# Seven block products in place of eight in part of two FFN down projections

## The chip, the cores and the metric

The program runs on one core of a Trainium2 chip. The core has TensorE for matrix products (called PE in the profile, with its weight loads listed apart as PEld), VectorE (DVE), ScalarE (ACT), GpSimd (POOL) and SyncE (SP), whose queue issues most of the DMAs. Each engine works through a queue of its own in order, and the engines wait for each other by semaphores. Products land in PSUM, eight banks of 128 partitions x 512 float32; everything else lives in SBUF, 128 partitions wide.

The metric is device time in microseconds for one execution of the whole program, as the median of several executions. Smaller is better. A TensorE product takes a stationary operand of 128 x 128 (the weights that PEld loads) and streams a moving operand of up to 512 columns past it.

## The reference

A decoder trunk of two layers on 512 tokens of width 1024, in float32. Layer 0 is a gated mixer, layer 1 is sliding-window attention; both are followed by the same kind of feed-forward block (FFN), which is where the change lies:

```python
def conv_ffn(xn, w_up, conv_w, conv_b, w_down):
    S = xn.shape[1]
    h = xn @ w_up
    hp = jnp.pad(h, ((0, 0), (CONV_WIDTH - 1, 0), (0, 0)))
    c = conv_b + sum(hp[:, t:t + S] * conv_w[t] for t in range(CONV_WIDTH))
    g, u = jnp.split(c, 2, axis=-1)
    return (jax.nn.silu(g) * u) @ w_down
...
        h = h + conv_ffn(rmsnorm(h, norm_ffn[i]), f_w_up[i], f_conv_w[i], f_conv_b[i], f_w_down[i])
```

`w_up` is 1024 x 5632 and `w_down` is 2816 x 1024 in each layer. After the FFN comes a gated per-layer embedding, and after layer 0 a shared key/value projection.

## The kernel before

**Layout.** Activations are kept transposed: a tile holds 128 features as partitions and the 512 tokens as columns. The residual stream `h` is eight such tiles. The 2816 inner features of an FFN are 22 tiles, numbered `j`.

**Three products for one.** Operands go into TensorE as float32r in two pieces: a high part (a cast) and a low part (the original less the cast). Each product of a weight block and an activation tile is three matmuls, high x high, high x low and low x high (`mm3`, lines 185 to 196), added up in PSUM. So each float32 block costs three weight loads and three passes of 512 columns.

**Weights.** Weight matrices come from HBM in *pieces* of up to 128 x 2048 float32 (1 MB), in one fixed order, into three raw buffers `r0` to `r2` used in turn (`load`, lines 130 to 141). `pump` (143 to 167) splits each piece into *units* of up to 1024 columns: ScalarE casts the high part `wh` (line 164), VectorE subtracts for the low part `wl` (line 165). There are four buffers each for `wh` and `wl` (`WBUFS`), and `chunk` (175 to 183) sends the splits four units ahead before it takes the units it needs. A split waits for TensorE to release a unit buffer; a DMA waits for the splits to release a raw buffer.

**The FFN** (`ffn`, 401 to 443) is done in three parts of 8, 7 and 7 inner tiles (`PARTS`). `up(j)` multiplies the gate and the value columns of tile `j` (2 x 24 matmuls of 512 columns, into two PSUM banks), and then runs the epilogue for each of the two: VectorE scales by the norm's factor (`hs`, line 417), ScalarE applies the first tap of the convolution (line 421), VectorE the two others (422 and 423); then SiLU on ScalarE (426), the product of the two on VectorE (427), and `split` (271 to 274) into the high and low operands `ah{j}` and `al{j}`. These live in nine slots of an arena. When the tiles of a part are done, and one tile of the next part has been computed ahead, `dense_add` (389 to 399) multiplies them by four pieces of `w_down`, 256 output features each: 2 x 3 matmuls of 512 columns for each inner tile, two PSUM banks, and two additions onto `h` by VectorE (397). In the last part each finished tile of `h` goes straight into the next norm (`norm.take`).

**The norm's factor** of an FFN takes a detour: `begin` and `rstd` send it through DRAM and back by two DMAs on GpSimd's queue while TensorE already runs the first `up`. The products are scaled afterwards, so TensorE doesn't wait for it, and VectorE does.

**The order.** The program is traced in the order in which the Python code runs; a scheduler then orders each engine's queue ahead of time, putting an instruction in when its inputs should be ready, and among several the one that was traced first. What the chip later makes of the waits doesn't change the order.

Of the kernel before, what the change touches and what calls it, by code (L numbers as in the profile page):

```python
# [8 lines left out]
F32 = mybir.dt.float32  # L9
# [10 lines left out]
NJ = FF // P  # L20
PARTS = [(0, 8), (8, 15), (15, 22)]
SLOTS = 9
# [26 lines left out]
def tile_yoco(ctx: ExitStack, tc: tile.TileContext, t, out: bass.AP, out_b: bass.AP):  # L49
# [7 lines left out]
    mp = ctx.enter_context(tc.tile_pool(name="mp", bufs=1))  # L57
    tp = ctx.enter_context(tc.tile_pool(name="tp", bufs=2))
    dram = ctx.enter_context(tc.tile_pool(name="dram", bufs=1, space=bass.MemoryType.DRAM))
# [6 lines left out]
    pieces, paired = [], set()  # L66

# [10 lines left out]
    def plan_cols(w, n_chunks, kk, cols=256, k0=0):  # L78
        for c in range(n_chunks):
            plan(w[c, :, k0 * cols : (k0 + kk) * cols], kk * cols, cols)  # L80

    def plan_pair(w, k0, k1, own=None):

        paired.add(len(pieces))
        plan(w[:, :, k0 * 256 : k1 * 256].rearrange("c p m -> p c m"), (k1 - k0) * S, S, own)

    def plan_ffn(l):
        for i, (j0, j1) in enumerate(PARTS):
            if i == 0:
# [8 lines left out]
            plan_cols(t["w_down"][l], 4, j1 - j0, k0=j0)  # L98

# [13 lines left out]
    plan_ffn(1)  # L113
    free = [j % SLOTS for j in range(NJ, NJ + 8)]
    for c in range(2):
# [4 lines left out]
    units = [(i, q, lo, n) for i, p in enumerate(pieces) for q, (lo, n) in enumerate(p[2])]  # L120
    raws, ready, splits = {}, {}, {}
    state = {"raw": 0, "unit": 0, "next": 0, "tags": [0, 1, 2], "turn": 0, "pt": 0, "sent": {}}

    def behind(ins, front):
# [3 lines left out]
                          reason="order")  # L128

    def load(upto, queue=nc.sync):  # L130
        while state["raw"] < min(upto, len(pieces)):
            j = state["raw"]
            a, m = pieces[j][:2]
            tags = state["tags"]
            r = wp.tile([P, 2 * UNIT], F32, tag=f"r{tags[state['turn'] % len(tags)]}", bufs=1, name=f"wraw{j}")
            state["turn"] += 1
            ins = queue.dma_start(r[:, :m].rearrange("p (c m) -> p c m", c=2) if j in paired else r[:, :m], a)
            for front in state["sent"].pop(j, []):
                behind(ins, front)
            raws[j] = r  # L140
            state["raw"] += 1

    def pump(upto):
        while state["unit"] < min(upto, len(units)):
# [10 lines left out]
            if i in paired:  # L155
# [28 lines left out]

    def mm3(ps, parts, xs, c0, n=P, first=True, last=True, lows_last=False):


        todo = []
        for (wh, wl, off), (xh, xl) in zip(parts, xs):
            hi, low = (w[:, off + c0 : off + c0 + n] for w in (wh, wl))  # L190
            todo.append([(hi, xh), (hi, xl), (low, xh)])
        if lows_last:
            todo = [[t[j] for t in todo for j in (0, 2)], [t[1] for t in todo]]
        todo = [x for t in todo for x in t]
        for j, (w, x) in enumerate(todo):
            nc.tensor.matmul(ps, w, x, start=first and j == 0, stop=last and j == len(todo) - 1)  # L196

# [191 lines left out]
    def dense_add(xs, kk, norm):  # L389

        for c in range(4):
            parts = chunk(256, kk)
            for j in range(2):
# [4 lines left out]
                if norm is not None:  # L398
                    norm.take(m)

    def ffn(l, norm, nxt):

# [3 lines left out]
        def up(j):  # L406
# [20 lines left out]
            nc.vector.tensor_mul(a, a, cs[1])  # L427
            hi = ap.tile([P, S], F32R, tag=f"ah{j % SLOTS}", name=f"ah{j}")
            lo = ap.tile([P, S], F32R, tag=f"al{j % SLOTS}", name=f"al{j}")
            split(a, hi, lo)  # L430
            return hi, lo

        act = [up(0)]
        pe = None
        for i, (j0, j1) in enumerate(PARTS):
            act += [up(j) for j in range(j0 + 1, j1)]
            last = j1 == NJ
            if last:
                pe = ple_in_rows() if l else ple_in(l)
            nact = [] if last else [up(j1)]  # L440
            dense_add(act, j1 - j0, nxt if last else None)
            act = nact
        return pe
# [199 lines left out]
    xkv, xq = nm.xs[0][0], nm.xs[1][0]  # L643
    at = ctx.enter_context(tc.tile_pool(name="at", bufs=1))


# [565 lines left out]
```

## Time and profile before

| | us |
|---|---|
| median of 3 executions | 1129.52 (1129.44 to 1129.74) |
| span of the profiled execution, first to last instruction | 1127.4 |
| TensorE busy in it | 1118.7 (99%) |
| VectorE busy | 753.9 (67%) |
| ScalarE busy | 511.7 (45%) |
| GpSimd busy | 105.8 (9%) |

A time of its own is not given for the profiled execution beside its span; the span lies 2.1 us under the median, which is what stands around the first and the last instruction.

In the groups of instructions, a row is one line of the code on one engine with one shape: count, total busy time, mean duration of one in ns, and what ended the idle time before them. TensorE's matmuls overlap, so their durations (389 ns for 512 columns) are longer than the distance from one start to the next, and that distance is what counts. The granted TensorE clock was 0.998 over the span.

| stage (layer 0) | us from the span's start |
|---|---|
| `up` 0 to 8 | 143.9 to 242.35 |
| down projection, part 1 (8 tiles) | 242.35 to 285.87 |
| `up` 9 to 15 | 285.87 to 362.03 |
| down projection, part 2 (7 tiles) | 362.03 to 400.11 |
| `up` 16 to 21, embedding product | 400.11 to 476.51 |
| down projection, part 3 (7 tiles) | 476.51 to 514.59 |

Layer 1 has the same stages from 705.06 on.

### The profile page before, as it was taken

How to read it: one execution, taken by the hardware profiler on the slowest of the kernel's cores; microseconds unless marked ns; L12 is line 12 of the kernel's file. 1: busy time of each engine (PE TensorE's matmuls, PEld its weight loads, DVE VectorE, ACT ScalarE, POOL GpSimd, SP SyncE). 2: the span in 40 equal slices, each digit the busy share in tenths (PEclk: the TensorE clock that was granted, in tenths of full speed). 3: DMA queues.
4: the chain of work that ended last, by engine and by line, in shares of the span. 5: the costliest groups of instructions: out<-in, count | busy, mean ns of one | idle time of the engine just before them, and what ended most of it. 6: DMA issues, size and time to landing. Idle time of an engine off the chain costs nothing.

```text
span 1127.4 us, 13285 instructions
## 1 busy us (share of the span) xinstructions
PE 1118.7 (99%) x5115; PEld 930.4 (83%) x5115; DVE 753.9 (67%) x1166; ACT 511.7 (45%) x808; POOL 105.8 (9%) x167
## 2 busy tenths in 40 slices
PE   9999999999999999999999999999999999999997
PEld 7888888888888888888888887888888888888886
DVE  6566438873577457656988997488736773675686
ACT  5634325541344234544656776255413432344543
POOL 2100210000000000012204451100000000000210
PEclk9999999999999999999999999999999999999999
DMA  9632313333232222333134224333222233224333
GB/s 323 102 117 75 112 47 112 112 112 112 75 103 83 100 107 89 99 112 112 49 101 131 76 57 154 111 106 105 99 110 96 82 103 112 78 86 144 111 101 80
DMA packets 35616, 118.29 MB, mean 105 GB/s; under 512 B 11800, under 2 KB 17440, under 8 KB 26080
## 3 DMA queue, kind: packets, MB, share of 16 engines
q1 hardware_dynamic: 34800, 116.19, 31.9%
q0 software_dynamic: 336, 0.79, 0.4%
q8 instruction: 40, 0.66, 0.3%
q10 hardware_dynamic: 416, 0.46, 0.1%
q14 instruction: 24, 0.20, 0.1%
HBM read 109.02 MB, written 2.11 MB: 99 GB/s over the span
## 4 chain that ended last, share of the span: by engine, by line
PE 95%; DVE 2%; issue 1%; ACT 1%; DMA 0%; POOLq 0%; POOL 0%; ACTq 0%
PE up L196 42%; PE d L196 25%; PE q L196 4%; PE gate L196 4%; PE u L196 4%; PE o L196 2%; PE gt L205 1%; PE v L205 1%; PE gt L206 1%; PE gt L207 1%; PE v L206 1%; PE v L207 1%; PE pin L196 1%; PE k L196 1%; PE s L613 1%
## 5 line engine op out<-in xcount | busy, mean ns | idle before, releaser
L165 DVE TENSOR_TENSOR wl<-wraw,wh 128x1024 fp32r<-128x1024 f32 (+1 forms) x198 | 238.1, 1205 | 117.9 <-ACT wh L164 117.6
L164 ACT CAST wh<-wraw 128x1024 fp32r<-128x1024 f32 (+2 forms) x197 | 201.3, 1026 | 233.2 <-PE d L196 129.9
L196 PE MATMUL up<-nf00h,wh 128*128 128x512 f32 x352 | 137.1, 390 | 0.0
L196 PE MATMUL up<-nf10h,wh 128*128 128x512 f32 x352 | 137.0, 389 | 0.0
L196 PE MATMUL up<-nf00h,wl 128*128 128x512 f32 x352 | 136.9, 389 | 0.0
L196 PE MATMUL up<-nf10h,wl 128*128 128x512 f32 x352 | 136.9, 389 | 0.0
L196 PE MATMUL up<-nf10l,wh 128*128 128x512 f32 x352 | 136.9, 389 | 0.0
L196 PE MATMUL up<-nf00l,wh 128*128 128x512 f32 x352 | 136.9, 389 | 0.0
L196 PE MATMUL d<-ah,wh 128*128 128x512 f32 x352 | 136.9, 389 | 0.0
L196 PE MATMUL d<-al,wh 128*128 128x512 f32 x352 | 136.9, 389 | 0.0
L196 PE MATMUL d<-ah,wl 128*128 128x512 f32 x352 | 136.9, 389 | 0.0
L421 ACT ACTIVATE c<-hs,vec 128x512 f32<-128x512 f32 x88 | 71.5, 815 | 91.6 <-DVE hs L417 89.4
L422 DVE SCALAR_TENSOR_TENSOR c<-hs,vec,c 128x511 f32<-128x511 f32 x88 | 65.7, 749 | 33.7 <-ACT c L421 33.6
L397 DVE TENSOR_TENSOR h<-h,d 128x512 f32<-128x512 f32 x56 | 38.4, 686 | 72.6 <-PE d L196 72.6
L196 PEld LDWEIGHTS up<-nf10h,wl 128*128 128x128 f32 x352 | 66.1, 188 | 13.8
L196 PEld LDWEIGHTS d<-ah,wh 128*128 128x128 f32 x352 | 66.1, 188 | 13.8
L196 PEld LDWEIGHTS up<-nf00h,wh 128*128 128x128 f32 x352 | 66.1, 188 | 13.7
L196 PEld LDWEIGHTS up<-nf00l,wh 128*128 128x128 f32 x352 | 66.1, 188 | 13.7
L196 PEld LDWEIGHTS d<-al,wh 128*128 128x128 f32 x352 | 66.1, 188 | 13.7
L196 PEld LDWEIGHTS d<-ah,wl 128*128 128x128 f32 x352 | 66.1, 188 | 13.7
L196 PEld LDWEIGHTS up<-nf10l,wh 128*128 128x128 f32 x352 | 66.1, 188 | 13.7
L196 PEld LDWEIGHTS up<-nf00h,wl 128*128 128x128 f32 x352 | 66.1, 188 | 13.7
(392 smaller groups left out, 1947.8 us busy)
## 6 DMA issues: line engine op xcount, KB each, us to landing
wraw<-in_w_up SPq DMA_DIRECT2D x44, 1024.0 KB, 4.8
wraw<-in_w_down SPq DMA_DIRECT2D x16, 896.0 KB, 4.6
wraw<-in_w_down SPq DMA_DIRECT2D x8, 1024.0 KB, 5.0
wraw<-in_w_gate SPq DMA_DIRECT2D x8, 1024.0 KB, 5.2
wraw<-in_w_u SPq DMA_DIRECT2D x4, 1024.0 KB, 8.0
wraw<-in_w_out SPq DMA_DIRECT2D x4, 1024.0 KB, 4.8
wraw<-in_w_q SPq DMA_DIRECT2D x4, 1024.0 KB, 5.2
wraw<-in_w_o SPq DMA_DIRECT2D x4, 1024.0 KB, 4.9
```

Of the source, the lines that this page charges most:

```text
L164: cast = nc.scalar.copy(hi, src)
L165: state["split"] = splits[u] = cast, nc.vector.tensor_sub(low, src, hi.bitcast(F32))
L196: nc.tensor.matmul(ps, w, x, start=first and j == 0, stop=last and j == len(todo) - 1)
L205: nc.tensor.matmul(ps, xh[:, s], wh[:, a:b], start=st, stop=False)
L206: nc.tensor.matmul(ps, xl[:, s], wh[:, a:b], start=False, stop=False)
L207: nc.tensor.matmul(ps, xh[:, s], wl[:, a:b], start=False, stop=en)
L397: nc.vector.tensor_add(h[m], h[m], ps)
L421: nc.scalar.activation(c, hs, AF.Identity, bias=v("conv_b", l * 2 * NJ + col), scale=cw[2])
L422: nc.vector.scalar_tensor_tensor(c[:, 1:], hs[:, : S - 1], cw[1], c[:, 1:], op0=ALU.mult, op1=ALU.add)
L613: nc.tensor.matmul(sp[:, b * P : (b + 1) * P], zv[b][:, m * P : (m + 1) * P], wsT[:, m, :], start=True, stop=True)
```

## The change

The down projections of the first two parts, now 8 tiles each (the last part keeps 6), are computed by a block scheme with seven products of half size in place of eight. A *pair* is two inner tiles `a` and `b`; its tokens are cut into two halves of 256, and the 256 output features of a piece of `w_down` are two tiles, `top` and `low`. That is a 2 x 2 block product, (inner tile) x (token half) against (inner tile) x (output tile), done with sums of blocks on both sides:

- On the activations, `Pair.begin(a)` and `Pair.end(b)` form `t = (a1 - a2, b2 - a2)` and `u = (-t1 - b2, -u1 + b1)`, indices being token halves, and split `b`, `t` and `u` in full and the first half of `a` (`edge`). `a` itself is no longer split in full.
- On the weights, `weave` forms four sums of blocks for each piece in three additions by VectorE. The sums take one of the three raw buffers in their turn. A piece is then split into four units: raw blocks, two units of sums, and half a unit of raw blocks, 3584 columns in place of 2048.
- `woven_add` replaces `dense_add` for these parts. A product P1 to P7 is 4 pairs x 3 matmuls of 256 columns. P1 starts a bank, `chain`, whose running value is read out by ScalarE after P1, P6, P7 and P4; P2 and P5 start the halves of another bank, `other`, and P3 goes onto P5's half after VectorE has subtracted P5 from `h`. P4 of a block of 256 outputs is put off (`late`) until after P6 of the next block.

```diff
-PARTS = [(0, 8), (8, 15), (15, 22)]
+PARTS = [(0, 8), (8, 16), (16, 22)]
...
+    def plan_woven(w, n_chunks, k0, k1):
+        for c in range(n_chunks):
+            n = (k1 - k0) * P
+            woven.add(len(pieces))
+            pieces.append((w[c, :, k0 * 256 : k1 * 256], 2 * n, [(0, n)] * 3 + [(0, n // 2)], None))
...
+    def weave(i, q):
+        n = pieces[i][1] // 4
+        g = raws[i][:, : 4 * n].rearrange("p (k b m) -> p b k m", b=4, m=P)
+        if q == 0:
+            s = sums[i] = staged(f"wsum{i}")[:, : 4 * n].rearrange("p (b k m) -> p b k m", b=4, m=P)
+            k = n // P
+            nc.vector.tensor_add(s[:, 0::3], g[:, 1:2].to_broadcast([P, 2, k, P]), g[:, 0::3])
+            nc.vector.tensor_add(s[:, 2], s[:, 3], g[:, 0])
+            nc.vector.tensor_add(s[:, 1], s[:, 2], g[:, 2])
+        return (g[:, 0:3:2], sums[i][:, 2:4], sums[i][:, 0:2], g[:, 3:4])[q]
...
+        def begin(self, a):
+            self.a = a
+            self.own, self.ones, self.twos = (couple(homes[3 * self.p + x], f"{self.name}_{x}") for x in range(3))
+            hi, lo = self.edge
+            nc.scalar.copy(hi, a[:, first])
+            self.t = tp.tile([P, S], F32, tag="acc", name=f"{self.name}t")
+            nc.vector.tensor_sub(self.t[:, first], a[:, first], a[:, second])
+            nc.vector.tensor_sub(lo, a[:, first], hi.bitcast(F32))
+
+        def end(self, b):
+            t, u = self.t, tp.tile([P, S], F32, tag="sq", name=f"{self.name}u")
+            nc.vector.tensor_sub(t[:, second], b[:, second], self.a[:, second])
+            nc.vector.scalar_tensor_tensor(u[:, first], t[:, first], -1.0, b[:, second],
+                                           op0=ALU.mult, op1=ALU.subtract)
+            nc.vector.scalar_tensor_tensor(u[:, second], u[:, first], -1.0, b[:, first],
+                                           op0=ALU.mult, op1=ALU.subtract)
+            for src, (hi, lo) in ((b, self.own), (t, self.ones), (u, self.twos)):
+                split(src, hi, lo)
...
+        def unit():
+            pump(state["next"] + WBUFS)
+            return take()
+
+        def product(x, ps, w, at0, first=True):
+            wh, wl = w[:2]
+            mm3(ps, [(wh, wl, at0 + k * P) for k in range(len(pairs))], ops[x], 0, first=first,
+                onto=not first)
+
+        def close(c, chain, w, tail):
+            def run():
+                product(4, chain, w, 0, first=False)
+                nc.scalar.copy(tail[:, first], chain)
+                nc.vector.tensor_sub(h[2 * c + 1], h[2 * c + 1], tail)
+            return run
+
+        late = None
+        for c in range(4):
...
+            w = unit()
+            product(1, chain, w, 0)
+            product(2, other[:, first], w, n)
+            nc.scalar.copy(head[:, first], chain)
+            w = unit()
+            product(5, other[:, second], w, n)
+            product(6, chain, w, 0, first=False)
+            nc.vector.tensor_sub(low[:, second], low[:, second], other[:, second])
+            nc.scalar.copy(head[:, second], chain)
+            w = unit()
+            if late:
+                late()
+            for x in (7, 3) if c == 3 else (3, 7):
+                if x == 3:
+                    product(3, other[:, second], w, n, first=False)
+                else:
+                    product(7, chain, w, 0, first=False)
+                    nc.scalar.copy(tail[:, second], chain)
+            nc.vector.tensor_add(top, top, head)
+            nc.vector.tensor_add(top, top, other)
+            late = close(c, chain, unit(), tail)
+        late()
...
+            if i < WOVEN:
+                edge = at.tile([P, PAIRS, 2, N], F32R, tag="vtl", name=f"edge{i}")
+                pairs = []
+                for p in range((j1 - j0) // 2):
+                    pair = Pair(p, edge, f"act{i}_{p}")
+                    pair.begin(up(j0 + 2 * p) if p else ahead)
+                    pair.end(up(j0 + 2 * p + 1))
+                    pairs.append(pair)
+                ahead = up(j1)
+                woven_add(pairs)
+                continue
```

More of the change, by code (lines that the diff above doesn't have):

```diff
@@ L113, in tile_yoco @@
     plan_ffn(1)
-    free = [j % SLOTS for j in range(NJ, NJ + 8)]
+    free = [(5 + j) % SLOTS for j in range(8)]
     for c in range(2):
@@ L154, in pump @@
                 wl = wp.tile([P, UNIT], F32R, tag="wl", bufs=WBUFS, name=f"wl{u}")
-            if i in paired:
+            if i in woven:
+                src = weave(i, q)
+                hi, low = (x[:, :n].rearrange("p (b k m) -> p b k m", b=src.shape[1], m=P) for x in (wh, wl))
+            elif i in paired:
                 whole = raws[i][:, : pieces[i][1]].rearrange("p (c k n) -> p k c n", c=2, n=256)
@@ L183, in chunk, with mm3 @@
         return parts
-    def mm3(ps, parts, xs, c0, n=P, first=True, last=True, lows_last=False):
+    def mm3(ps, parts, xs, c0, n=P, first=True, last=True, lows_last=False, onto=False):
         todo = []
@@ L195, in mm3 @@
         for j, (w, x) in enumerate(todo):
-            nc.tensor.matmul(ps, w, x, start=first and j == 0, stop=last and j == len(todo) - 1)
+            nc.tensor.matmul(ps, w, x, start=first and j == 0, stop=last and j == len(todo) - 1,
+                             skip_group_check=onto)
     def mm3t(ps, xs, parts, c0, n, tok, first=True, last=True):
@@ new lines, in woven_add @@
+    def woven_add(pairs):
+        ops = {x: [p.operand(x) for p in pairs] for x in range(1, 8)}
+        n = len(pairs) * P
+        def unit():
[13 more added lines that the diff above has]
+        for c in range(4):
+            top, low = h[2 * c], h[2 * c + 1]
+            chain, other = psum(f"dx{c}")[:, first], psum(f"dy{c}")
+            head = tp.tile([P, S], F32, tag="acc", name=f"head{c}")
+            tail = tp.tile([P, S], F32, tag="sq", name=f"tail{c}")
+            w = unit()
[13 more added lines that the diff above has]
+                    product(3, other[:, second], w, n, first=False)
+                else:
+                    product(7, chain, w, 0, first=False)
[4 more added lines that the diff above has]
+        late()
```

56 lines of the change are left out of this document (39 added, 17 removed).

## The prediction

> **What bounds the kernel now.** I read the page's busy times first, then the chain that ended last in order of time, then the matmuls one by one, and last VectorE's queue around the FFN. The page:
>
> ```profile
> span 1127.4 us, 13285 instructions
> PE 1118.7 (99%) x5115; PEld 930.4 (83%) x5115; DVE 753.9 (67%) x1166; ACT 511.7 (45%) x808; POOL 105.8 (9%) x167
> ...
> PE 95%; DVE 2%; issue 1%; ACT 1%; DMA 0%; POOLq 0%; POOL 0%; ACTq 0%
> ```
>
> The chain's pieces (start, us, engine, tile):
>
> ```profile
> 242.35 43.52 PE d L196 x192
> 285.87 76.16 PE up L196 x336
> 362.03 38.08 PE d L196 x168
> ...
> 803.24 43.52 PE d L196 x192
> ```
>
> TensorE is the bound: in both FFN the chain stays on it without a break, 43.52/192 = 226.7 ns from one matmul of 512 columns to the next. What leaves TensorE there leaves the span, unless something else becomes late.
>
> **TensorE's part of the change.** Taken out: 2 layers x 16 tiles x 4 pieces x 2 output tiles x 3 = 768 matmuls of 512 columns, 768 x 226.7 ns = 174.1 us. Put in: 2 layers x 2 parts x 4 pieces x 7 products x 4 pairs x 3 = 1344 matmuls of 256 columns. That shape stands in the shared values projection, 128 x 128 weights, another one each time (timeline of TensorE, first and last of 72 in a row):
>
> ```profile
> 580.88 0.28 PE L206 MATMUL vv<-wh,n10l 128*128 128x256 f32 x1
> ...
> 589.40 0.28 PE L205 MATMUL vv<-wh,n10h 128*128 128x256 f32 x1
> ```
>
> (589.40 - 580.88)/71 = 120.0 ns. So 1344 x 120.0 ns = 161.3 us, a gain of **12.8 us**, and a block of 256 outputs takes 84 x 0.120 = 10.08 us of TensorE in place of 48 x 0.2267 = 10.88. It is 7% and not an eighth because 120 is more than half of 226.7; at 129.5 ns nothing would be left.
>
> The Trainium skill, in TensorE: Matmul & The Clock Gate, section Back-to-back issue gap, gives N/2.4 + 2.5 ns between warm matmuls, an estimate of 109 and 216 ns for the two shapes; by that the gain would be 165.7 - 146.8 = 18.9 us. Both rows are some 11 ns above it here, so the rows stand.
>
> **What VectorE and ScalarE get in exchange.** The prices, from the groups of instructions with shapes kept apart (mean ns last before the idle time):
>
> ```profile
> L165 DVE TENSOR_TENSOR wl<-wraw,wh 128x1024 fp32r<-128x1024 f32 x178 | 220.0, 1238 | 108.2 <-ACT wh L164 108.0
> L397 DVE TENSOR_TENSOR h<-h,d 128x512 f32<-128x512 f32 x56 | 38.4, 686 | 72.6 <-PE d L196 72.6
> L740 DVE SCALAR_TENSOR_TENSOR vt<-vv,n1rows,vt 128x256 fp32r<-128x256 f32 x4 | 1.9, 482 | 1.5 <-ACT vt L739 1.5
> L1050 DVE TENSOR_TENSOR st<-st,pet 128x256 f32<-128x256 f32 x2 | 0.9, 426 | 0.6 <-ACT st L1041 0.6
> L164 ACT CAST wh<-wraw 128x1024 fp32r<-128x1024 f32 x178 | 186.0, 1050 | 216.9 <-PE d L196 122.9 <-PE up L196 59.0 <-PE gate L196 9.6
> L272 ACT CAST ah<-a 128x512 fp32r<-128x512 f32 x44 | 27.4, 622 | 106.5 <-DVE a L427 106.4
> L1049 ACT ACTIVATE st<-zt 128x256 f32<-128x256 f32 x1 | 0.4, 404 | 0.0
> ```
>
> And VectorE's own timeline in layer 0, from the first `up` to the first down projection, which carries the rest of the argument:
>
> ```profile
> 153.49 1.23 DVE L165 TENSOR_TENSOR wl<-wraw,wh 128x1024 fp32r<-128x1024 f32 x1 [3.03 <-ACT wh L164]
> 166.17 1.29 DVE L417 TENSOR_TENSOR hs<-up,nf0rstd 128x512 f32<-128x512 f32 x2 [11.45 <-DMA nf0rstd<-nf0line]
> 167.37 1.22 DVE L165 TENSOR_TENSOR wl<-wraw,wh 128x1024 fp32r<-128x1024 f32 x1
> ...
> 194.27 1.22 DVE L165 TENSOR_TENSOR wl<-wraw,wh 128x1024 fp32r<-128x1024 f32 x1
> 195.41 0.68 DVE L417 TENSOR_TENSOR hs<-up,nf0rstd 128x512 f32<-128x512 f32 x1
> ...
> 198.76 0.69 DVE L427 TENSOR_TENSOR a<-a,c 128x512 f32<-128x512 f32 x1
> 200.14 0.69 DVE L273 TENSOR_TENSOR al<-a,ah 128x512 fp32r<-128x512 f32 x1 [0.69 <-ACT ah L272]
> 200.75 0.68 DVE L417 TENSOR_TENSOR hs<-up,nf0rstd 128x512 f32<-128x512 f32 x1
> 202.32 0.75 DVE L422 SCALAR_TENSOR_TENSOR c<-hs,vec,c 128x511 f32<-128x511 f32 x1 [0.89 <-ACT c L421]
> 203.10 0.75 DVE L423 SCALAR_TENSOR_TENSOR c<-hs,vec,c 128x510 f32<-128x510 f32 x1
> ...
> 209.64 0.69 DVE L273 TENSOR_TENSOR al<-a,ah 128x512 fp32r<-128x512 f32 x1 [0.69 <-ACT ah L272]
> ...
> 246.57 0.69 DVE L427 TENSOR_TENSOR a<-a,c 128x512 f32<-128x512 f32 x1
> ```
>
> From start to start a subtraction of 1024 columns costs 195.41 - 194.27 = 1.14 us, one of 512 0.61 (200.14 to 200.75), and, taking the same 0.08 of overlap off, one of 256 0.35 and a two-step operation of 256 (L740's shape) 0.41, or 0.45 and 0.51 where the next one needs its result (start to start 0.78 at 203.10 for 0.75 before).
>
> *In the blocks of 256 outputs* VectorE gets: weave 1.14 + 2 x 0.61 = 2.36; four low parts 3 x 1.14 + 0.61 = 4.03; onto `h` 0.35 + 3 x 0.61 = 2.18. Together 8.57 us of 10.08, where before it had 2 x 1.14 + 2 x 0.61 = 3.5. ScalarE gets 3 x 1.05 + 0.62 for the casts and 4 x 0.40 for PSUM copies, 5.4 of 10.08; it is no bound. Neither is the work that TensorE waits for as such: ScalarE's copy of `chain` has a product or more (1.44 us) between the two products that it separates, and takes 0.40.
>
> *In the pairs*: before, from a tile's `a` to the next `hs` are 198.76 to 200.75 = 1.99 us. The first of a pair now takes 0.69, 0.47 of wait for a ScalarE copy of 256 (404 ns and the 0.07 that the old wait has beyond its cast of 622; the first subtraction lies inside), 0.35: 1.51. The second takes 0.71, the three chained operations 0.45 + 0.51 + 0.41, and three low parts 1.83: 3.91. A pair costs VectorE (1.51 + 3.91) - 2 x 1.99 = +1.44 us, in the time of two `up` of 10.88 us.
>
> *DMAs*: w_down's pieces stay 24, with the same bytes, and land as before:
>
> ```profile
> wraw<-in_w_down SPq DMA_DIRECT2D x8, 1024.0 KB, 5.0
> ```
>
> The sums take every other raw buffer, so a piece's DMA in SP's queue waits until the sums of the piece two before are split. That is done by P3 of that piece's block, 7.2 us into it; with 5.0 to land the piece is there 12.2 us in, and its own block begins at 20.2. I cost it at nothing: the 8 us of slack hide it, and only what a split is later than that would be paid. Nothing in SP's queue is reordered.
>
> **Where the lateness arises.** The timeline shows VectorE idle for 11.45 us at the head of each FFN, because `hs` stands in its queue and waits for the norm's factor; a weight split stood behind it. From then on VectorE runs as fast as its own chain lets it, 209.64 - 200.14 = 9.50 us for an `up` that lasts 10.88 on TensorE, of which it is idle 0.69 + 0.89 in waits for ScalarE. Its last `a` before the down projection still ends at 246.57 + 0.69 = 247.26, 4.9 us after TensorE began the down projection at 242.35. That was harmless: the next thing TensorE wants from it comes later. It isn't in the new order. P3 goes onto P5's bank after VectorE's subtraction, and in the first block no `late` stands between, so P3 is due after 48 matmuls, at 242.35 + 5.76 = 248.1, and the subtraction stands in VectorE's queue behind the whole epilogue.
>
> Stall in part 1 of layer 0: 247.26 + four pairs 5.8 + weave of the first piece (2.36, of which the 0.89 gaps of earlier `up`s may take most; between 0.3 and 2.4, I take 1.3) - 0.5 (one of two weight splits before it is now 512 wide) = 253.9 for the last `a`. Between it and the subtraction stand none or all of the next piece's weave and first low part, traced earlier, 0 to 3.5 us; I take half, 1.75. With the subtraction's 0.43: 256.1. **8.0 us** (5.2 to 10.8). Layer 1 has the same picture:
>
> ```profile
> 806.95 0.69 DVE L427 TENSOR_TENSOR a<-a,c 128x512 f32<-128x512 f32 x1
> ```
>
> This is 3.7 us after 803.24, against 4.2 in layer 0: **7.5 us** (4.7 to 10.3). In part 2 VectorE isn't late:
>
> ```profile
> 362.07 0.69 DVE L417 TENSOR_TENSOR hs<-up,nf0rstd 128x512 f32<-128x512 f32 x1 [0.64 <-PE up L196]
> ...
> 365.22 0.69 DVE L427 TENSOR_TENSOR a<-a,c 128x512 f32<-128x512 f32 x1
> ```
>
> Its last `a` ends 365.91 - 362.03 = 3.9 us into the down projection; with up to 3.5 and 0.43 behind it the subtraction ends between 4.8 (P5 ends at 4.3) and 7.8, P3 is due at 5.76: 0 to 2.0, I take 1.5, twice: **3.0**. In the other 12 blocks `late` leaves 2.88 us after P5, and a weave with the subtraction takes 2.36 + 0.35 = 2.71: **0**, but one low part more in front of it would cost 1.0 a block, 12 us in all. Inside the `up`s TensorE's weights keep a margin: in the old trace the low part at 203.77 follows 9.50 us after that at 194.27, and a pair's 1.44 spread over two `up`s leaves 10.2, under 10.88.
>
> Sum: -12.8 + 8.0 + 7.5 + 3.0 = +5.7 us on the span of 1127.4, so 1133.1, and with the 2.1 us between it and the median of 1129.5, **1135.2 us**.
>
> **Rivals.**
>
> *Faster, the gaps take the work.* If the scheduler puts the pairs' operations into the two gaps of 1.58 us per `up` (12.6 us in eight), VectorE reaches the down projection no later than now, and 12.8 us are gained less some 0 to 6: 1116.7 to 1123, say 1119. For it: 67% busy VectorE and these gaps. Against: in the old queue the gap of 0.89 (row at 202.32) stays empty although two weight splits stand in each `up`. It decides at 6.4 us of stall per layer.
>
> *Slower, VectorE becomes the bound inside the blocks.* At 8.57 of 10.08 us any ordering that leaves it idle for 1.5 us in a block is paid by TensorE: 12 blocks by 1.0 on top of the above, 1147. For it: four of its eleven operations in a block wait for a cast of ScalarE. Against: a unit's buffer is free after P2, 2.88 us into a block, and wanted again at 10.08, so the casts have 7 us.
>
> *Weight loads show.* If a load couldn't hide behind 256 columns, the row of loads would set the distance:
>
> ```profile
> L207 PEld LDWEIGHTS vv<-wl,n10h 128*128 128x128 f32 x32 | 6.1, 192 | 0.0
> ```
>
> 1344 x 192 - 174.1 = +84 us, 1213. The 72 matmuls at 120.0 ns beside these very loads speak against it. The same page of the Trainium skill, section The mechanism, says that a load overlaps matmuls in flight only where its row group differs, which would forbid the overlap here; this trace disagrees.
>
> **How the numbers follow.** A difference of 0.2%, 2.3 us, is about what a measurement of this kernel can tell from none. The late VectorE 0.62: its bounds give -12.8 + 9.9 + 0 = -2.9 to -12.8 + 25.1 = +12.3, so 1126.6 to 1141.8, its own range; of the 0.62, 0.53 are slower, 0.05 the same, 0.04 faster. The gaps 0.25, faster. VectorE the bound 0.12 and the loads 0.01, slower. Faster 0.29, same 0.05, slower 0.66. For 8 in 10 the range takes in most of the gap case and the start of the bound case: 1118 to 1147.
>
> **What would show it.** TensorE: 1344 matmuls of 256 columns, 120 ns apart. In the first block of part 1 in each layer a gap on TensorE before P3, ended by VectorE's subtraction from `h`, of 5 to 11 us; in part 2 one under 2. The `up`s without gaps on TensorE. VectorE some 135 us busier by the mean durations: 16 x (2.6 for the sums, 1.9 for splits, 2.9 for a pair, 1.1 onto `h`). I am wrong if TensorE runs through these first blocks, if the distance isn't 120, or if the stalls repeat in every block.

## The result, and the profile after

The changed kernel is slower, by 0.3%: 1131.99 us median (1130.16 to 1135.53, 20 executions) beside 1129.30 (1128.64 to 1129.87, 20 executions) for the kernel before on the same chip, a ratio of **1.0028, 95% interval 1.0021 to 1.0035**. I had predicted 1135.2. The profiled execution took 1133.61 us, 1.6 more than the median, so its trace shows somewhat more than the median contains. The page of the changed kernel:

```profile
span 1131.6 us, 14890 instructions
...
PE 1111.8 (98%) x5691; PEld 949.7 (84%) x5691; DVE 869.2 (77%) x1374; ACT 569.1 (50%) x936; POOL 105.2 (9%) x167
...
PE 79%; DVE 15%; issue 2%; ACT 2%; DMA 1%; POOL 0%; POOLq 0%; ACTq 0%; DVEq 0%
```

TensorE has less work than before (1111.8 us busy against 1118.7), and the span is longer all the same. The chain was on TensorE for 95% of the span before, and is for 79% now; VectorE has taken 15%. By the starts of TensorE's matmuls the 4.2 us of span come from these stretches (a down projection or a gate begins with its first matmul):

| stretch | before | after | difference |
|---|---|---|---|
| start to the down projection of layer 0, part 1 | 242.19 | 242.01 | -0.18 |
| from there to the gate of layer 0 | 272.24 | 271.89 | -0.35 |
| gate of layer 0 to the down projection of layer 1, part 1 | 288.65 | 292.94 | **+4.29** |
| from there to the gate of layer 1 | 272.32 | 272.37 | +0.05 |
| rest | 52.00 | 52.39 | +0.39 |

So the two FFN came out even, and the loss lies between them, where the change put nothing.

**Inside the FFN.** A part of eight tiles took 43.52 us. In block products it takes 45.37 and 41.27 us in layer 0, 45.75 and 41.29 in layer 1; 336 x 120.0 ns are 40.32. What a part takes beyond that I call its stall: 5.05, 0.95, 5.43 and 0.97, together 12.4 us of the 12.8 gained. TensorE's timeline at the first block of part 1, the same place in layer 1, and in part 2 of layer 0:

```profile
246.92 0.39 PE L229 MATMUL dx<-act_2h,wh 128*128 128x256 f32 x1 [0.47 <-ACT head L509]
...
248.46 0.40 PE L229 MATMUL dx<-edge,wh 128*128 128x256 f32 x2
248.70 0.28 PE L229 MATMUL dy<-act_0h,wh 128*128 128x256 f32 x1
248.82 0.28 PE L229 MATMUL dy<-act_0l,wh 128*128 128x256 f32 x1
251.94 0.58 PE L229 MATMUL dx<-edge,wl 128*128 128x256 f32 x1 [2.84 <-DVE wl L198]
252.32 0.41 PE L229 MATMUL dx<-act_1h,wh 128*128 128x256 f32 x1
252.53 0.41 PE L229 MATMUL dx<-act_1l,wh 128*128 128x256 f32 x1
...
816.91 0.39 PE L229 MATMUL dx<-edge,wl 128*128 128x256 f32 x1 [2.71 <-DVE wl L198]
...
381.51 0.39 PE L229 MATMUL dx<-edge,wl 128*128 128x256 f32 x1 [0.71 <-DVE wl L198]
```

The first matmuls of the *next* block's P1 (`edge`, 248.46) stand in TensorE's queue ahead of P3 of the first block, because the scheduler took them to be ready. The wait of 2.84 us is for the low part of that next piece, not for the subtraction from `h`. VectorE's timeline shows both, one behind the other, and how late it is; the three rows above them are for the price of a pair:

```profile
178.69 0.69 DVE L555 TENSOR_TENSOR a<-a,c 128x512 f32<-128x512 f32 x1
183.20 0.75 DVE L550 SCALAR_TENSOR_TENSOR c<-hs,vec,c 128x511 f32<-128x511 f32 x1 [0.29 <-ACT c L549]
198.18 0.69 DVE L555 TENSOR_TENSOR a<-a,c 128x512 f32<-128x512 f32 x1
...
250.07 0.68 DVE L555 TENSOR_TENSOR a<-a,c 128x512 f32<-128x512 f32 x1
250.67 1.22 DVE L198 TENSOR_TENSOR wl<-wraw,wh 128x1024 fp32r<-128x1024 f32 x1
251.80 0.41 DVE L513 TENSOR_TENSOR h<-h,dy 128x256 f32<-128x256 f32 x1
```

The last `a` ends at 250.75, 8.7 us after TensorE began the down projection; before it was 4.9. The low part of the next piece follows at once, and TensorE goes on when that is done. The subtraction from `h` ends at 252.21, 0.3 us later, so P3 without P1 in front of it would have waited about as long.

Behind the gap the matmuls are 0.21 us apart instead of 0.12 until 254.84. In the table of stretches (us, busy time and count of PE, PEld, DVE, ACT and POOL, granted clock, DMA share, GB/s) the whole of part 1 in layer 0, the 2.9 us behind the gap, and the whole of part 2:

```profile
242.00:287.40 45.40, 42.09 (x338) 41.61 (x337) 37.12 (x49) 22.05 (x36) 0.00 (x0) 0.96 0.34 120
251.90:254.80 2.90, 2.86 (x13) 2.86 (x14) 2.05 (x3) 0.00 (x0) 0.00 (x0) 0.51 0.00 0
374.40:415.70 41.30, 40.59 (x337) 40.29 (x337) 34.45 (x46) 20.76 (x33) 0.00 (x0) 1.00 0.38 131
```

The granted clock fell to 0.51 after a gap of 2.84 us. The 13 matmuls of that stretch took 2.9 us in place of 13 x 0.120 = 1.6: **1.3 us** lost that no row of waits shows. The Trainium skill, in TensorE: Matmul & The Clock Gate, section What's actually happening, has the clock halved after an idle window of about 3.4 us whose phase runs free. This trace agrees on the half, but a gap of 2.84 us was enough here. In layer 1 the clock was halved for 3.41 us too, from 817.97 on, and the 17 matmuls in it cost 1.4 us.

**Between the FFN.** SP's queue, which issues the loads, of the changed kernel:

```profile
658.45 0.33 SPq L167 DMA_DIRECT2D wraw<-in_w_o  x1
679.86 0.33 SPq L167 DMA_DIRECT2D wraw<-in_w_up  x1
685.22 0.33 SPq L167 DMA_DIRECT2D wraw<-in_w_o  x1
```

and of the kernel before:

```profile
656.53 21.73 SPq L137 DMA_DIRECT2D wraw<-in_w_o  x2
683.26 20.44 SPq L137 DMA_DIRECT2D wraw<-in_w_up  x4
```

Before, the last two pieces of `w_o` are issued one after the other, the last at 677.9. After, the first `up` piece of layer 1 goes ahead of the last `w_o` piece, which is issued at 685.22. The cause is the turn of the three raw buffers: eight sums move it on by eight, which is two modulo three, so the last `w_o` piece gets another buffer, one that attention still holds (SP waits 5.2 us there, until TensorE's `pv` has read it); experiment 1 shows it. And a second load is late. ScalarE's timeline, first of the kernel before:

```profile
605.75 2.00 ACT L164 CAST wh<-wraw 128x1024 fp32r<-128x1024 f32 x2 [1.09 <-DMA wraw<-in_w_q]
```

and of the changed one:

```profile
607.78 2.00 ACT L197 CAST wh<-wraw 128x1024 fp32r<-128x1024 f32 x2 [3.62 <-DMA wraw<-in_w_q]
```

The last piece of `w_q` was issued at 599.7 (600.2 before) and landed after 8.0 us instead of 5.5. TensorE itself goes on at first. The delay reaches it further on in attention, where before it had no such gap:

```profile
630.23 0.41 PE L1012 MATMUL tr<-ident,prs 128*128 128x128 f32 x2 [1.17 <-DVE prs L997]
```

From the gate of layer 0 to the first matmul with `w_o` TensorE takes 133.47 us instead of 131.35, so 2.1 of the 4.29 us are lost there.

### The profile page after: what moved, and what is told of

It is laid out like the page before. It is cut to its first block, busy times and chain, and to the rows that moved or that the text cites. A ratio compares the mean times of both kernels' runs of the same rounds, so it can differ in the third digit from the quotient of the medians.

```text
span 1131.6 us, 14890 instructions
## 1 busy us (share of the span) xinstructions
PE 1111.8 (98%) x5691; PEld 949.7 (84%) x5691; DVE 869.2 (77%) x1374; ACT 569.1 (50%) x936; POOL 105.2 (9%) x167
## 4 chain that ended last, share of the span: by engine, by line
PE 79%; DVE 15%; issue 2%; ACT 2%; DMA 1%; POOL 0%; POOLq 0%; ACTq 0%; DVEq 0%
PE up L229 30%; PE d L229 9%; PE dx L229 7%; PE dy L229 5%; DVE wl L198 4%; PE gate L229 4%; PE u L229 4%; PE o L229 3%; PE q L229 3%; DVE c L550 2%; DVE hs L545 1%; DVE c L551 1%; PE v L239 1%; PE v L241 1%; PE v L240 1%
## 5 line engine op out<-in xcount | busy, mean ns | idle before, releaser
L198 DVE TENSOR_TENSOR wl<-wraw,wh 128x1024 fp32r<-128x1024 f32 (+2 forms) x198 | 232.9, 1181 | 89.5 <-ACT wh L197 88.8
L197 ACT CAST wh<-wraw 128x1024 fp32r<-128x1024 f32 (+2 forms) x197 | 193.7, 989 | 150.3 <-PE up L229 53.6
L229 PEld LDWEIGHTS up<-nf10h,wh 128*128 128x128 f32 x352 | 66.1, 188 | 13.5
L551 DVE SCALAR_TENSOR_TENSOR c<-hs,vec,c 128x510 f32<-128x510 f32 x88 | 65.7, 748 | 2.3
L197 ACT CAST wh<-wsum 128x1024 fp32r<-128x1024 f32 x32 | 33.5, 1048 | 39.7 <-PE dx L229 21.4
L545 DVE TENSOR_TENSOR hs<-up,nf0rstd 128x512 f32<-128x512 f32 x44 | 30.1, 686 | 22.4 <-PE up L229 11.5
L545 DVE TENSOR_TENSOR hs<-up,nf1rstd 128x512 f32<-128x512 f32 x44 | 30.1, 687 | 22.1 <-PE up L229 11.0
L198 DVE TENSOR_TENSOR wl<-wsum,wh 128x1024 fp32r<-128x1024 f32 x32 | 39.1, 1222 | 6.1 <-ACT wh L197 6.1
L554 ACT ACTIVATE a<-c 128x512 f32<-128x512 f32 x44 | 27.8, 631 | 18.8 <-DVE c L551 18.7
```

The lines of the kernel that those rows point to most:

```text
L197: cast = nc.scalar.copy(hi, src)
L198: state["split"] = splits[u] = cast, nc.vector.tensor_sub(low, src, hi.bitcast(F32))
L545: nc.vector.tensor_mul(hs, ps, rstds[1])
L551: nc.vector.scalar_tensor_tensor(c[:, 2:], hs[:, : S - 2], cw[0], c[:, 2:], op0=ALU.mult, op1=ALU.add)
L554: nc.scalar.activation(a, cs[0], AF.Silu)
```

## The experiments

The traces gave two theories. A: the order of the two loads, and through it 1.85 us of the loss between the FFN, comes from the turn of the raw buffers and not from the block products themselves. L: the stall of part 1 is VectorE's lateness, which begins at the norm's factor; its rival is that the block products' own work on VectorE and their order make the stall. Times are medians of 4 to 11 executions, ratios are against the kernel before on the same chip.

**1. The turn of the buffers, undone and alone.** Changed kernel, and kernel before, each with one line where attention gives the three buffers back:

```diff
 # changed kernel
     state["tags"] = [0, 1, 2]
+    state["turn"] += 1
```

```diff
 # kernel before
     state["tags"] = [0, 1, 2]
+    state["turn"] += 2
```

> The changed kernel, with the turn of the three raw buffers moved on by one when attention hands them back, so that the last piece of w_o goes into the same buffer as in the kernel before. Theory A (the eight buffers that layer 0's sums take shift the turn by 8, two modulo 3; the last w_o piece lands in the buffer that attention's value tile holds to the end, its load starts 5.4 us later, and layer 1 starts 1.9 us later): 1.9 us less than the changed kernel, some 1.0007 of the kernel before; the load of the last w_o piece is issued right after the split of the third, ahead of the first load for layer 1's up. Theory B (attention is longer only because a w_q load took 2.5 us longer to land in that one execution): no difference from the changed kernel, 1.0024 or so.

> The kernel before, with only that turn moved on by two at the same place (8 modulo 3). Theory A: slower than the kernel before by about 1.9 us, 1.0017, with the last w_o load issued behind the first load for up. Theory B: no difference, within 0.0005.

Undone: 1131.09 us (1130.49 to 1133.52), 1.0019 (1.0010 to 1.0028). Alone: 1131.02 us (1130.53 to 1131.36), 1.0015 (1.0007 to 1.0024), and gate to down projection takes 290.50 us, +1.85, with the last `w_o` piece issued at 683.63 behind `up` at 678.24. The order of two loads is worth 1.85 us of span and has nothing to do with block products. Undone, that stretch takes 290.17 us: 2.8 of the 4.29 are gone, and 1.5 are left with the late `w_q` (ScalarE waits 2.97 us). In the median only 0.9 came back, not 1.9. The execution that was traced, itself at the median, lost more inside part 1: 46.95 and 44.57 us, 0.4 more than the changed kernel's two together. The gaps there are 2.84 and 2.71 us again, yet the clock is halved for 6.83 us after the one and not at all after the other. The stretches of the changed kernel on both sides of 251.35 and 817.97, where its clock fell:

```profile
247.94:251.35 3.41, 1.16 (x10) 0.95 (x8) 3.41 (x6) 1.32 (x2) 0.00 (x0) 1.00 0.40 166
251.35:254.77 3.42, 2.83 (x13) 2.83 (x14) 2.60 (x4) 0.00 (x0) 0.00 (x0) 0.50 0.00 0
...
814.55:817.97 3.42, 1.05 (x9) 1.06 (x10) 3.42 (x5) 0.72 (x2) 0.00 (x0) 1.00 0.00 0
817.97:821.38 3.41, 3.41 (x19) 3.41 (x18) 1.65 (x3) 0.00 (x0) 0.00 (x0) 0.50 0.00 0
```

and of the kernel with the turn undone, the stretch ahead of the half clock in layer 0, the half clock, and two stretches around the gap in layer 1:

```profile
247.93:251.34 3.41, 1.51 (x13) 1.31 (x11) 3.41 (x7) 1.55 (x3) 0.00 (x0) 1.00 0.48 202
251.34:258.17 6.83, 5.89 (x27) 5.89 (x28) 3.65 (x5) 0.32 (x1) 0.00 (x0) 0.50 0.00 0
...
811.13:814.54 3.41, 2.16 (x16) 1.96 (x16) 3.41 (x6) 2.34 (x4) 0.00 (x0) 1.00 0.68 274
814.54:817.95 3.41, 1.81 (x15) 1.82 (x16) 3.41 (x5) 0.00 (x0) 0.00 (x0) 1.00 0.00 0
```

In mid-kernel the clock of these traces changes in a fixed step: the half clock lasts 3.41 us twice and 6.83 once, and the 566.6 us between the two falls of the changed kernel are 166 steps of 3.4133. In the step ahead of each of the three falls TensorE was idle for 2.26, 2.36 and 1.90 us (3.41 less its busy time). Counted on from 258.17 in these steps, layer 1 of the second kernel has a step's border at 814.54, in the middle of its gap: 1.25 us of idle time lie in one step and 1.60 in the next, and the clock stays. So, by these four gaps, what counts is the idle time within one step, and the same gap costs or not by where it falls.

**2. The norm's factor without the way through DRAM.** In `ffn`, in both kernels:

```diff
-                    rstds.append(norm.rstd() if s else norm.begin(rows=0, halves=False, line=True))
+                    rstds.append(norm.rstd() if s else norm.begin(rows=0))
```

> The changed kernel, with the FFN's norm factor spread by one TensorE product and a ScalarE copy in place of two DMAs through DRAM, so that VectorE can start the epilogues some 10 us earlier. Theory L (part 1's first block stalls because VectorE enters it late from the wait for the factor): the stalls of part 1, 5.0 us in layer 0 and 5.4 in layer 1 with the half clock after them, shrink to part 2's 0.95 each; -8.5 us, 1.0024 - 0.0075 = 0.995. Rival D (the first block of a part stalls by its own design, whenever VectorE comes): part 1 keeps 4 us or more in each layer, time within 2 us of the changed kernel.

> The kernel before with the same short way for the norm factor. Theory L: the wait was covered there, TensorE had no gap behind it; 0 to -0.2 us plus the two added products, ratio 0.9995 to 1.0005. If it gains several us by itself, the gain of the changed kernel with it says nothing on the first blocks.

The changed kernel falls to **1125.10 us** (1124.28 to 1125.55), 0.9961 (0.9948 to 0.9973), its span by 8.1 us. The kernel before takes 1130.02, 1.0005 (0.9996 to 1.0014): to it the late VectorE had cost nothing. Part 1 now takes 41.26 and 41.29 us like part 2. TensorE's timeline of the changed kernel with this edit, layer 0:

```profile
248.82 0.28 PE L229 MATMUL dy<-act_0l,wh 128*128 128x256 f32 x1
249.81 0.39 PE L229 MATMUL dx<-edge,wl 128*128 128x256 f32 x1 [0.71 <-DVE wl L198]
```

The wait is at the same matmul, 0.71 us instead of 2.84, and the clock stays at 1.00 over the part. On VectorE the last `a`:

```profile
247.94 0.69 DVE L555 TENSOR_TENSOR a<-a,c 128x512 f32<-128x512 f32 x1
```

TensorE began this down projection at 242.75, so `a` ends 5.9 us into it instead of 8.7. The detour of the norm's factor makes VectorE 2.8 us later, and TensorE's waits in this block are 0.71 us without it and 0.47 + 2.84 = 3.31 with it. The rest of the lateness stays and costs no more than in part 2.

**3. Only part 2 in block products.** The changed kernel, `up` as it was; the last line, inside `weave`, keeps the turn of the raw buffers as before (4 + 8 = 12):

```diff
-            if i < WOVEN:
+            if i == 1:
...
+            if i == 0:
+                ahead = up(j1)
+                dense_add(act, j1 - j0, None)
+                continue
...
+            if len(sums) == 4:
+                state["turn"] += 8
```

T and W in the expectation are two theories on the late `w_q`, tried in experiment 4: by T it too comes from the turn of the raw buffers, by W it comes with the block products.

> The changed kernel with only the second part as block products; the first has its eight tiles in full products, and the norm's factor goes through DRAM as before. The turn is moved on by 8 at the fourth sum (4 + 8 = 12). If the stalls of part 1 come only from a VectorE that the norm's factor has made late, part 2 keeps its 41.28 us in place of 43.52 in each layer and nothing else moves: -4.5 us, 1124.8, ratio 0.9960 under T, 1126.8 and 0.9978 under W. If the stall belongs to the first woven part wherever it stands, part 2 takes 45.4 us and the time is about 1133.

1124.75 us (1124.41 to 1125.59), 0.9962 (0.9949 to 0.9974), and part 2 takes 41.17 and 41.26 us. Where VectorE isn't late the block products pay 2.3 us a part with the old norm, and half of the change brings as much as all of it did in experiment 2. (That run still has the two losses between the FFN; here the `w_q` cast waits only 0.84 us, and the order of the loads is the old one.) The time is the one that T gave, and W missed it by 2.1 us; experiments 4 and 6 show that T is wrong all the same, and why `w_q` isn't late here.

**4. The turn of the buffers, from layer 0 on.** The turn had already been another at `w_q`, which experiment 1 didn't touch: in SP's queue the second piece of `w_kv` stands before the second of `w_q`, before it was the other way round. The kernel before with that turn, and the kernel of experiment 2 with the old one:

```diff
 # kernel before, in load
+            if j == gates:
+                state["turn"] += 8
```

```diff
 # changed kernel with the edit of experiment 2, in weave
+            if len(sums) == 8:
+                state["turn"] += 4
```

> The kernel before, with the turn of the raw buffers moved on by 8 at the gate of layer 0, as the eight sums of layer 0 leave it in the changed kernel. In SP's queue the second piece of w_kv then stands ahead of the second piece of w_q, and the last piece of w_o behind the first of up. Theory T (both the late landing of w_q, some 2 us, and the late w_o, 1.85 us, come from the turn of the raw buffers, and nothing of it from the block products): +3.9 us, about 1133.2, ratio 1.0034; ScalarE's cast of w_q waits about 3 us instead of 1.1. Rival W (the late landing of w_q comes with the block products): only the w_o part, +1.85 us, 1131.1, 1.0016, and the cast waits about 1 us.

> The changed kernel with the norm's factor spread by a product, and with the turn of the raw buffers moved on by 4 at the eighth sum, so that from there on it is the one of the kernel before (8 + 4 is a multiple of 3 and of 2). T: both losses between the two FFN go, 3.85 us below the run with the factor alone (1125.1): 1121.3, ratio 0.9930. W: only the 1.85 us of w_o: 1123.3, 0.9945.

1130.81 us (1130.44 to 1131.38), 1.0013 (1.0004 to 1.0022), and 1123.26 us (1121.58 to 1123.76), 0.9945 (0.9932 to 0.9957). Both are what W gives, and theory T falls: the kernel before with the new order casts `w_q` after a wait of 0.61 us, the changed one with the old order after 2.60. The late landing isn't the turn's.

**5. The subtraction ahead.** The last kernel with

```diff
-            nc.vector.tensor_sub(low[:, second], low[:, second], other[:, second])
+            with tc.high_priority():
+                nc.vector.tensor_sub(low[:, second], low[:, second], other[:, second])
```

> As the run with the factor by a product and the turn moved on by 4, with the subtraction of P5 from h put ahead in VectorE's queue (high priority). The queue of TensorE changes with it: P6 and P3 of the first block come ahead of the next block's P1. If the stall of 0.95 us that is left at the head of each of the four parts comes from the order of those VectorE instructions, it goes: -3.8 us against that run, 1117.5 under T, ratio 0.9896. If it is only what VectorE's epilogue is behind TensorE at that place, the wait moves to another product: within 0.8 us of that run.

**1119.43 us** (1117.74 to 1120.15), 0.9908 (0.9893 to 0.9923), 3.8 us less than without it. The four parts take 40.41, 40.58, 40.42 and 40.31 us, within 0.3 of their matmuls. TensorE's timeline, first block of layer 0:

```profile
247.69 0.28 PE L231 MATMUL dx<-act,wl 128*128 128x256 f32 x1
247.81 0.28 PE L231 MATMUL dy<-act_0h,wh 128*128 128x256 f32 x1
...
249.13 0.28 PE L231 MATMUL dy<-act,wl 128*128 128x256 f32 x1
249.26 0.38 PE L231 MATMUL dx<-act_1h,wh 128*128 128x256 f32 x1
```

P3 (`dy<-act_0h`, 247.81) follows P6 with no gap, and the next block's P1 no longer stands ahead of it. The subtraction and TensorE's order moved together, so which of the two removes the wait isn't shown apart. This is the fastest version, and it beats both kernels. From the gate of layer 0 to the down projection of layer 1 it still takes 290.75 us, 2.1 more than the kernel before; the late `w_q` is in that.

**6. Why `w_q` lands late.** In experiments 1 to 5 the late landing is in every kernel with both parts in block products, and in none of the others. A view of the DMA queues for the microsecond after the issue of the last `w_q` piece in the changed kernel (queue, packets, MB, share of 16 engines):

```profile
q1 hardware_dynamic: 4, 0.03, 15.2%
q8 instruction: 1, 0.02, 13.9%
```

One packet of a queue called instruction begins just ahead of the piece's own, 0.8 us after the issue, and 13.9% of 16 engines for 1.00 us are 2.2 us of one engine. In the kernel before it comes 8.1 us after the issue. It seems to be TensorE's: the pages of the two kernels count 40 such packets for 2 x 5115 matmuls and weight loads (256 each) and 44 for 2 x 5691 (259 each). The Trainium skill, in Runtime: NRT & Kernel Launch, section Instruction fetch mechanics, says that an engine's instructions are refilled in blocks of 256 by a DMA queue of the sequencer's own, mostly hidden; the counts agree. The block products add 288 matmuls to layer 0, and 288 = 2 x 128 + 32, so the packets come 32 matmuls, some 7 us, earlier. One part in block products adds 144 = 128 + 16, and in experiment 3 the packet comes 4.4 us after the issue, about half as much earlier. So 32 more idle matmuls at the program's start should move the packet onto `w_q` in the kernel before, and off it in the kernel of experiment 5:

```diff
-IDLE = 9
+IDLE = 41
...
-        nc.tensor.matmul(ps, idle, idle.rearrange("p (o t) -> p o t", o=1).to_broadcast([P, 4, P]),
+        nc.tensor.matmul(ps[:, :, :22], idle, idle[:, :22].rearrange("p (o t) -> p o t", o=1).to_broadcast([P, 4, 22]),
```

> The kernel before, with the nine idle matmuls of 512 columns at the start of TensorE's queue as 41 of 88: as much idle work, 32 more instructions ahead of all others. Theory F: the last piece of w_q lands late where a packet of TensorE's instructions is loaded by one of the DMA engines just as that piece begins to move; in the kernel before the packet comes 7.8 us after the piece's issue, in the kernels with both parts in block products, which have 32 matmuls more modulo 128, 0.8 us after it or less. With 32 matmuls more the packet here moves to about 601, 0.8 us after the issue at 600.2: ScalarE's cast of w_q waits some 3 us in place of 1.1, and the time is 2.0 us longer, 1131.1, ratio 1.0018. Rival: the late landing has to do with the block products in another way; 1129.1 as before, within 0.5, and the cast waits about 1 us.

> The run with the subtraction put ahead, with the same 41 idle matmuls. F: the packet moves from 595.5 to about 588.5, after the first of the two pieces has landed and before the second is issued: the cast waits about 1 us in place of 2.98, and the time is 2.0 us shorter than that run, 1117.4, ratio 0.9897. Rival: 1119.4, within 0.5, and the cast waits about 3 us.

The total times are no use: 1137.28 us (ratio 1.0072, 1.0059 to 1.0085) and 1125.32 (0.9966, 0.9952 to 0.9979), because the first down projection of layer 0 begins 6.7 and 5.9 us later. 41 idle matmuls of 88 columns take 8.8 us and not the 4.0 of nine of 512, and behind them TensorE runs at half speed for longer (last section). The idle work isn't the same, and that part of my expectation was wrong. But the stretch in question lies 500 us later. The kernel before with the idle matmuls, ScalarE:

```profile
614.13 2.00 ACT L164 CAST wh<-wraw 128x1024 fp32r<-128x1024 f32 x2 [2.77 <-DMA wraw<-in_w_q]
```

its DMA queues from 607.6 to 608.6, where the piece was issued at 606.9:

```profile
q1 hardware_dynamic: 18, 0.15, 79.2%
q8 instruction: 1, 0.02, 8.4%
```

the kernel of experiment 5 without the idle matmuls, ScalarE:

```profile
602.21 2.01 ACT L199 CAST wh<-wraw 128x1024 fp32r<-128x1024 f32 x2 [2.98 <-DMA wraw<-in_w_q]
```

and with them:

```profile
606.07 1.05 ACT L199 CAST wh<-wraw 128x1024 fp32r<-128x1024 f32 x1 [0.56 <-DMA wraw<-in_w_q]
```

The wait goes from 1.09 to 2.77 us in the one and from 2.98 to 0.56 in the other, as the packet moves. From the gate of layer 0 to the first `up` of layer 1 the kernel before then takes 191.88 us instead of 190.46 (+1.42), the other 190.87 instead of 192.27 (-1.40). Theory F holds, in both directions, at 1.4 us and not the 2.0 I gave. All twelve traces agree: the packet begins 0.7 to 1.5 us after the issue in six, and there the piece lands after 7.0 to 8.0 us; in the other six it comes 4.4 us or more after the issue, or 5.7 ahead of it, and the piece lands after 4.9 to 5.5. Why one engine's 1 to 2 us become 2 or more at the piece's end stays open. A version with the packet moved at no cost wasn't tried.

## Why the prediction was right or wrong

The direction was right, and the reason I gave, a VectorE that is late because of the norm's factor, was shown by experiment 2: it took 8.1 us off the span of the changed kernel and nothing off the kernel before. But that reason alone only ate the gain; what makes the kernel slower than before comes on top. The terms of the sum:

- **The gain of 12.8 us: right.** Blocks without a stall take 10.08 us, and with all stalls gone (experiment 5) a part takes 40.31 to 40.58 us against 40.32 worked out.

```profile
267.30 2.87 PE dy L229 x24
270.18 2.88 PE dx L229 x24
```

  These are pieces of the chain of the changed kernel: 24 matmuls of 256 columns in 2.87 us, 120 ns. The weight-load rival is out.
- **The stall of part 1, 8.0 and 7.5 us: too large, and at another place.** It was 5.05 and 5.43, just under the lower bound in layer 0. The step by which P3 is due after 48 matmuls and waits for the subtraction failed in part: I took TensorE's order from the code, and the scheduler had put the next block's P1 ahead of P3, which waits for the low part of the next piece. That cost almost nothing, since the subtraction came 0.3 us after that low part. The size went wrong on VectorE: the last `a` ended at 250.75 instead of 253.9, and the subtraction 1.5 us later instead of 2.2. Experiment 5 shows that the two orders matter for the last 0.95 us of a part.
- **The price of a pair, 1.44 us: about 0.7.** From the second `a` of a pair to that of the next are 198.18 - 178.69 = 19.49 us, then 20.97 and 18.83; before, 19.00, 19.00 and 19.30. In the first of them the scheduler put the next `hs` between the pair's operations, and `c` waits 0.29 us instead of 0.89 (row at 183.20). So the rival in which the gaps take the work was partly right. The weave and the end of the fourth pair cost more than I gave them: to the last `a` are 12.09 us instead of 9.51. From the first to the last `a` of the part VectorE lost 4.6 us, where I had 6.6; it had also started 1.1 us earlier.
- **Missed: the clock.** 1.3 us of the 5.05 in layer 0 and 1.4 of the 5.43 in layer 1 are matmuls at half the clock behind the gap, so what VectorE's lateness cost by itself was smaller still, 3.8 and 4.0. It includes a wait of 0.47 us for ScalarE's copy of `chain` (row at 246.92; 0.76 in layer 1), which I had ruled out.
- **Part 2, 1.5 each: 0.95 and 0.97**, in the range; it is the wait of 0.71 us and what surrounds it.
- **Other blocks 0: right**, and VectorE did not become the bound at 8.57 of 10.08 us. It was 115 us busier, where I had 135.
- **The step that failed worst: "I cost it at nothing ... Nothing in SP's queue is reordered."** I looked at the down projections' own loads, which are indeed not late. But the sums take turns of the raw buffers, and the phase of that turn stays changed long after the last sum. It reordered two loads 270 us later, for 1.85 us (experiments 1 and 4). I had not counted where each later piece lands.
- **Missed: the instruction packet**, 1.4 us where it alone was moved (experiment 6) and 2.1 in the changed kernel. The order of the loads has nothing to do with it (experiment 4).

Put together, the stalls came to 12.4 us, which is 6.0 and 6.4 a layer; 6.4 is the point from which I had said that the sign turns. By stalls alone the change would have been a wash, and the slowdown that I predicted came about through two losses outside the FFN that I had priced at nothing. Too large a stall and two missing terms cancelled in part, so the sign of the result was in part luck.

The executions of the changed kernel lie between 1130.16 and 1135.53 us; with the gap of 0.71 us (experiment 2) they lie within 1.3 us. The clock behind the long gaps, which was halved for 0, 3.4, 3.4 and 6.8 us in two traces, would give such a spread. The granted clock of each execution agrees: it was 0.997 to 0.998 in the four fastest (1130.16 to 1130.68 us) and 0.993 to 0.994 in the four slowest (1134.70 to 1135.53). 0.004 of 1131 us are 4.5 us, an estimate, and the two groups are 4.7 apart. No run changed the clock alone.

## What to carry to other kernels

When a change takes turns in a shared ring of buffers, work out the phase of the ring for everything behind it, not only for the change's own loads; a count that is a multiple of the ring's length leaves the rest alone. A delay that costs nothing, here VectorE behind the norm's factor, is a debt that the next change may have to pay: look for it before moving work onto that engine, and remove it first. And read an engine's real order from the trace once there is one, since in a queue fixed ahead of time what stands first waits first.

## What the runs showed of the hardware

- The granted clock changed in steps of 3.41 us (experiment 1). It was halved after a step in which TensorE had been idle for 1.90 to 2.36 us, three times, in gaps of 2.84 and 2.71 us. It was not halved after another gap of 2.71, whose idle time lay 1.25 and 1.60 us in two steps. After gaps of 0.71 it stayed at 1.00 (experiment 2). At half the clock matmuls of 256 columns lie 0.21 us apart instead of 0.12, so 6.83 us of it cost 2.7 us, as much again as the gap.
- Loads of TensorE's instructions get in the way of weight loads. 1.4 us were lost when one such packet of 16 KB began with a 1 MB load that ScalarE's cast was waiting for, and the number of matmuls ahead decides whether it does (experiment 6).
- Behind 256 columns weight loads are hidden at 120 ns. At the start of the kernel of experiment 5 with idle matmuls, the groups of instructions show 88 columns, and TensorE's timeline shows what comes behind them:

```profile
L280 PE MATMUL idle<-idle 128*128 128x88 f32 x41 | 9.0, 422 | 1.1 <-DVE minus_half L283 1.1
L280 PEld LDWEIGHTS idle<-idle 128*128 128x128 f32 x41 | 8.8, 332 | 1.1 <-DVE minus_half L283 1.1
...
10.89 1.05 PE L666 MATMUL v<-wl,n00h 128*128 128x512 f32 x2
11.74 0.94 PE L666 MATMUL v<-wh,n00l 128*128 128x512 f32 x2
12.52 0.63 PE L666 MATMUL v<-wh,n00h 128*128 128x512 f32 x2
12.99 0.62 PE L666 MATMUL v<-wl,n00h 128*128 128x512 f32 x2
```

  41 matmuls of 88 columns took 8.8 us, 214 ns each, with weight loads on the whole time, so here the loads aren't hidden. But TensorE was at half speed: the matmuls of 512 columns behind them lie (11.74 - 10.89)/2 = 0.43 us apart, and from 12.5 us on 0.23. Whether 88 columns hide a load at full speed isn't shown.
